# Two cache copies from DRAM to DRAM, issued in the third pair from the end and no longer among the first attention loads

## The chip, the cores and the metric

The kernel runs on one core of a Trainium2 chip. The metric is device time of one execution in microseconds (us). The engines are PE (matrix products), DVE (vector work), ACT (activations, copies and casts), POOL, and SP, which here does nothing but issue transfers. Each engine runs its own instructions in order; engines wait for one another and for transfers by semaphores.

## What is computed

One inference step of a hybrid layer on 1024 prompt tokens and on 8 samples of 4 tokens (32 sample tokens): 1024 features, an mLSTM branch with 4 heads and an attention branch with 8 query and 2 key/value heads of 64, over a window of 128 positions.

```
h = rmsnorm(x, g) * (1 + scale) + shift            # scale, shift, gate from c
mq, mk, mv, mi, mf, mo, mz, aq, ak, av, az, gm, ga = split_in(h @ w_in)
y_m, C, n, m = mlstm_branch(...)                   # gated by sigmoid(mo) * silu(mz)
k = partial_rope(ak); v = av
kk = concatenate([cache_k, k]); vv = concatenate([cache_v, v])      # samples
o = sink_attend(q, kk, vv, ...)
k_sample, v_sample = kk[:, -128:], vv[:, -128:]
y_a = o * silu(az)
x = x + gate * ((sigmoid(gm) * (y_m @ w_mo) + sigmoid(ga) * (y_a @ w_ao)) @ w_o)
```

The part that matters here is `k_sample` and `v_sample`: of each sample's 128 cached rows the last 124 are kept and its 4 new rows follow. Nothing in the step reads these two outputs again.

## The kernel before

**Products.** Matrix products in fp32 are made of two parts: each weight tile is split into a rounded part `wh` (a cast on ACT) and the rest `wl` (a subtraction on DVE), each input likewise into `h_h` and `h_l`, and three matmuls stand for one product: `h_h` with `wh`, `h_l` with `wh`, `h_h` with `wl`. Every matmul is recorded at L275, every instruction of ACT and DVE at L220, every transfer at L261 (`dma` and `issue`, L254 to L270).

**First stage.** Up to about 130 us PE makes the attention's projections (`g_aq` for the queries) column group by column group. Between them it runs side work, generators that are stepped when they are due. `kv_turn` (L797) is one: it turns the new values (`avn`, to DRAM as `vnD`), writes the outputs `v_p` and `k_p` and the samples' `k_s` and `v_s`. The queries go to DRAM (`qD<-aqr`), come back in the layout that attention needs (`uqv<-qD`, `ukv<-kD`, `uqv<-vnD`), and the first unit of attention multiplies them (`sc<-ukv,uqv`). In the same queue run the weights (`wr_aq`, `wr_mk`) and those of the conditioning (`adar_ga`).

**Pairs.** Then come 18 pairs of projection columns, by `block_products` (L1520): 4 of the mLSTM inputs, 8 gates, 2 of the attention's output gates, and 4 `head_gate` pairs, one per mLSTM head, each of one block of `mo` and one of `mz`. A pair takes seven products of weight combinations, in the order 5, 6, 2, 7, then product 1 of the next pair, then 3 and 4. A weight in the trace is named by its product (`wh_phead_gate_5` is product 5 of a `head_gate` pair) and a running number. Before each product `hook(n, i)` is called with the pair's number and the product's, and product 5 of a pair loads the four weight tiles of the next (`wr_mo` and `wr_mz`, two each, 256 KB a tile, from a ring of 9 buffers). `wh` and `wl` come from rings of 4 buffers each: a cast waits until PE has done with the tile four casts back.

Results lie in PSUM banks of four pools with 2 banks each. The pool `pg` holds `bx` and `bw`. Product 2 ends the use of `bx` (ACT takes the result out: `hg<-bx`), and product 1 of the next pair, two products later, writes the same bank again:

```
flat += [(n, i) for i in (5, 6, 2, 7)] + nx if n else ...
elif i == 2:
    job_.done(0, 0, X)          # hg<-bx
if i == 1:
    o = NX = bank(pg, "bx")
```

**Order.** PE's instructions are chained in the order of the code. In this stage the order on ACT, DVE and SP is made by a scheduler, from its own estimate of when each becomes ready, so that an instruction which moves can move others. Transfers are further held by `paced`: until the last but one pair, each SP transfer is put behind the PE instruction that stands last in the code when it is issued. The writes of results (`ymD<-hg`, `ymD<-gts`) are collected by `store` and issued 8 us of estimated PE time later; `ho<-yhD` loads what the mLSTM heads left in DRAM.

Of the kernel before, what the change touches and what calls it, by code (L numbers as in the profile page):

```python
# [173 lines left out]
def body(tc, a):  # L174
    nc = tc.nc
    with ExitStack() as ctx:
# [11 lines left out]
        def pb(shape, name):  # L188
            return ps.tile(shape, F32, tag="b", bufs=2, name=name)
# [4 lines left out]
        def ht(shape, name, dt=F32):  # L194
            return sp.tile(shape, dt, tag="half", bufs=50, name=name)
# [51 lines left out]
        def stores(src=None):  # L247

            for e in list(due):
                if e[0] <= side.now or (src is not None and e[1].tensor is src):  # L250
                    due.remove(e)
                    issue(*e[1:])

        def dma(out, in_, late=False):  # L254
            stores(in_.tensor)
            issue(out, in_, late)
# [3 lines left out]
        def issue(out, in_, late=False, eng=None):  # L260
            ins = (eng or nc.sync).dma_start(out, in_)  # L261
            ins = getattr(ins, "ins", ins)
            if eng is None and paced:
                no_sync(ins, [last["PE"]])
            if late:
                no_sync(ins, free)
                free.clear()
            free.append(ins)
# [8 lines left out]
        def tr(out, in_, idn):  # L277
            side.now += 0.11
            side.products += 1
            in_order(nc.tensor.transpose(out, in_, idn))  # L280
# [516 lines left out]
        def kv_turn():  # L797
            kl, kTs, vT, kns, vns = at.pop("kl"), at["kTs"], at.pop("vT"), ht([128, 128], "kns")[:NS], at["vns"]
            for p, n in enumerate((3, 3, 2)):
                tp = pb([128, 3, 128], f"vtp{p}")  # L800
                for j in range(n):
                    tr(tp[:, j], vT[p][:, j * 128:(j + 1) * 128], ident)
                vn = ht([128, 3, 128], f"avn{p}")
                S.copy(vn[:, :n], tp[:, :n])
                dma(vnD[:, 3 * p:3 * p + n], vn[:, :n])
                if p < 2:
                    yield 4.0, "b"
            dma(a["v_p"], vn[:, 1])
            tp = pb([128, 3, 128], "kvtp")
            tr(tp[:, 0], kl[:, 128:256], ident)  # L810
            tr(tp[:NS, 1], kTs, ident)
            tr(tp[:NS, 2], vT[2][:, 256:288], ident)
            kn = ht([128, 128], "kl")
            V.tensor_copy(kn, tp[:, 0])
            V.tensor_copy(kns, tp[:NS, 1])
            V.tensor_copy(vns, tp[:NS, 2])
            dma(a["k_p"], kn)
            dma(a["k_s"][0:124], a["cache_k"][4:128])
            dma(a["v_s"][0:124], a["cache_v"][4:128])
            dma(a["k_s"][124:128].rearrange("t b e -> b t e"), kns)  # L820
            dma(a["v_s"][124:128].rearrange("t b e -> b t e"), vns)

# [673 lines left out]
        class head_gate:  # L1496
# [14 lines left out]
            def samples(self, o):  # L1511
# [6 lines left out]
                store(ymD[h][:, SEQ:T], t[:, 0])  # L1518

        def block_products(jobs, hook):  # L1520
            flat = [(0, 1)]
            for n in range(len(jobs)):
# [25 lines left out]
            for j, (n, i) in enumerate(flat):  # L1548
                job_ = jobs[n]
                nxt = jobs[n + 1] if n + 1 < len(jobs) else None  # L1550
                hook(n, i)
                if i == 3 and not nxt:
                    job_.samples_end()
# [55 lines left out]
        def att_sums(k):  # L1609

            def part(n, t):
                if n in ROOM:
                    hi, lo = [y[:, ROOM.index(n), 512 * k:512 * k + 512] for y in ymt]
                else:
                    hi, lo = [ht([128, 512], f"ya{n}{x}{k}", F32R) for x in "hl"]
                ya[n][k] = hi, lo
                S.copy(hi, t)
                (G if (n, k) in ASIDE else V).tensor_tensor(lo, t, hi.bitcast(F32), op=ALU.subtract)

            ts = []  # L1620
            for i, f in ((k, 0), (2 + k, 1), (k, 1), (2 + k, 0)):
                ts.append(ht([128, 512], "yr"))
                dma(ts[-1], yaD[i][:, HALF[f]])
            b11, b22, b12, b21 = ts
            yield 6.0, ""
            src = {"b11": b11, "t2": b11, "b21": b21, "t4": b21, "b22": b22, "t3": b22, "t1": b12}
            less = {"t3": (b22, b12), "t1": (b12, b11), "t4": (b21, b11)}
            for n in (("b22", "t3", "b21", "b11", "t1", "t2", "t4"), ("b11", "b22", "t3", "t1", "t2", "b21", "t4"))[k]:
                while n in ROOM and not ymt:
                    yield 0.3, ""  # L1630
                if n in less:
                    x, y = less[n]
                    V.tensor_tensor(x, x, y, op=ALU.subtract)
                elif n == "t2":
                    V.tensor_tensor(b11, b11, b22, op=ALU.add)
                part(n, src[n])
                yield LAG, ""
# [289 lines left out]
        for p, (c0, n) in enumerate(PARTS):  # L1927
            if p == 2:
                dma(hD[:, :, SEQ:T], xS)
            else:  # L1930
                for k in range(KT):
                    dma(hD[:, k, c0:c0 + n], xT[p][k])
        side.add("m", gates(gp, zg, gbias), "")
        side.add("a", kv_turn(), "b")
        V.on = S.on = False
        paced.append(True)
# [84 lines left out]
        pairs = [Pair(head_in, i) for i in range(len(paired))] + [Pair(gate, d) for d in range(KT)] + [Pair(query_gate, i) for i in range(2)] + [Pair(head_gate, h) for h in range(NH)]  # L2021

        def hook(n, i):
            if n == 0 and i in (6, 5):
                side.until(lambda: {6: "t2", 5: "t1"}[i] in formed)
            if i == 6:
                if pairs[n].kind is query_gate:
                    side.until(lambda: len(units_done) == 16)
                side.until(lambda: len(samples_done) >= {head_in: 0, gate: 0, query_gate: 1, head_gate: pairs[n].i + 2}[pairs[n].kind])
            if (n, i) == (OUT_WEIGHTS, 6):  # L2030
                side.add("g", out_weights())
            if (n, i) in LOADS:
                side.add("x", att_sums(LOADS.index((n, i))))
            if n == len(pairs) - 1:
                next(att, None)
            if n == len(pairs) - 2:
                paced.clear()
            if (n, i) == (10, 7):
                begun.append(4)

        OUT_WEIGHTS = 5
        LOADS = [(len(pairs) - 2, 7), (len(pairs) - 1, 5)]
        work = block_products(pairs, hook)
        att = att_products()
        side.add("g", ada_gate())
# [163 lines left out]
        for i, r in enumerate(blocks_of_rows):  # L2209
# [69 lines left out]
            else:  # L2279
# [9 lines left out]
                for f, (y, (c0, n)) in enumerate(zip(Y, parts)):  # L2289
                    r.product(4, y, False, c0, n)  # L2290
                    c = slice(c0, c0 + n)
# [85 lines left out]
```

## Time and profile before

| | |
|---|---|
| median of the runs | 823.43 us (3 runs, 823.28 to 824.55) |
| the profiled execution | 823.38 us |
| its span, first to last instruction | 821.6 us |
| mean granted clock of PE | 0.997 |
| busy: PE, DVE, ACT, POOL | 803.5, 598.6, 419.5, 45.8 us |
| transfers, mean rate | 165.49 MB, 201 GB/s |
| the two copies | 496 KB each, issued at 72.37 and 80.33 us |

The times in the text are those of the profiled execution, counted from the start of its span. "PE 90%" in the profile's chain that ended last says that nine tenths of the time are a sequence of PE instructions; the rest of a view's columns are named where it is quoted. Matmuls overlap: one of 512 columns is recorded as 0.39 us long and the next begins 0.23 us behind its start.

### The profile page before, as it was taken

The numbers are of one execution on the slowest core, as the hardware profiler recorded it, in microseconds if no ns is written. First come the engines' busy times: TensorE is split into PE (matmuls) and PEld (weight loads), VectorE is DVE, ScalarE is ACT, GpSimd is POOL, SyncE is SP. The second block draws the span as 40 slices with busy tenths as digits, with TensorE's granted clock in tenths as the row PEclk, the third lists the DMA queues.
The fourth block names the chain that finished last, engine by engine and source line by source line (L and its number), as shares of the span: only waits on it lengthen the run. The fifth ranks groups of instructions, "written<-read, shape, count | busy, mean of one in ns | idle before, by whom it ended". The sixth has DMA issues, their size and how long they took to land.

```text
span 821.6 us, 15097 instructions
## 1 busy us (share of the span) xinstructions
PE 803.5 (98%) x5145; PEld 666.4 (81%) x5145; DVE 598.6 (73%) x1495; ACT 419.5 (51%) x1020; POOL 45.8 (6%) x111
## 2 busy tenths in 40 slices
PE   6999999999999999999999999999999999999996
PEld 3779898888788878888888878788888789997775
DVE  4799886756755557475657889898668997876666
ACT  5764355656565564546555545554446652224334
POOL 0120000000000000000001011010002101000000
PEclk9999999999999999999999999999999999999998
DMA  9995756546545415437765685864435789647632
GB/s 332 374 333 159 227 164 211 178 153 212 171 138 174 145 59 160 160 136 255 238 213 145 238 265 184 265 217 141 141 104 179 241 303 375 228 137 284 205 104 109
DMA packets 113473, 165.49 MB, mean 201 GB/s; under 512 B 21184, under 2 KB 55744, under 8 KB 113364
## 3 DMA queue, kind: packets, MB, share of 16 engines
q1 hardware_dynamic: 107748, 153.78, 56.9%
q10 hardware_dynamic: 4176, 6.56, 2.2%
q0 software_dynamic: 1472, 4.20, 1.4%
q8 instruction: 40, 0.66, 0.3%
q14 instruction: 37, 0.30, 0.1%
HBM read 115.51 MB, written 50.00 MB: 201 GB/s over the span
## 4 chain that ended last, share of the span: by engine, by line
PE 90%; DVE 5%; DMA 2%; issue 2%; ACT 1%; SPq 0%; DVEq 0%; ACTq 0%
PE by L275 12%; PE bx L275 11%; PE bw L275 11%; PE g_w_mo L275 6%; PE bz L275 5%; PE g_mq L275 3%; PE g_aq L275 3%; PE foW L275 3%; PE foX L275 2%; PE foY L275 2%; PE smp L275 2%; PE sc L275 2%; PE oT L275 2%; PE pt L280 2%; PE n L275 2%
## 5 line engine op out<-in xcount | busy, mean ns | idle before, releaser
L220 ACT ACTIVATE p<-p,nmx 128x256 f32<-128x256 f32 (+1 forms) x64 | 31.1, 486 | 17.7 <-DVE nmx L220 17.7
L220 DVE CUSTOM_DVE_ANT_0 p<-sc,cst,sink 128x256 f32<-128x256 f32 (+1 forms) x64 | 26.1, 462 | 9.2 <-PE sc L275 9.1
L275 PE MATMUL g_aq<-h_h,wh_aq 128*128 128x384 f32 (+1 forms) x96 | 32.2, 336 | 0.0
L275 PE MATMUL g_aq<-h_h,wl_aq 128*128 128x384 f32 (+1 forms) x96 | 30.9, 322 | 0.0
L275 PE MATMUL g_aq<-h_l,wh_aq 128*128 128x384 f32 (+1 forms) x96 | 30.9, 321 | 0.0
L275 PE MATMUL g_w_mo<-ym_h,wh_w_mo 128*128 128x384 f32 (+1 forms) x96 | 30.8, 321 | 0.0
L275 PE MATMUL g_w_mo<-ym_l,wh_w_mo 128*128 128x384 f32 (+1 forms) x96 | 30.8, 321 | 0.0
L275 PE MATMUL g_w_mo<-ym_l,wl_w_mo 128*128 128x384 f32 (+1 forms) x96 | 30.8, 321 | 0.0
L220 DVE COPY p<-pt 128x512 f32<-128x512 f32 (+1 forms) x16 | 10.5, 657 | 16.9 <-PE pt L280 16.8
L220 ACT CAST wosh<-wor 128x512 fp32r<-128x512 f32 x24 | 14.8, 621 | 12.6 <-DVE wor L220 12.6
L275 PEld LDWEIGHTS g_aq<-h_h,wh_aq 128*128 128x128 f32 x96 | 18.0, 188 | 2.5 <-issue 1.5
L261 POOL DMA_DIRECT2D oD<-uqv x16 | 8.8, 552 | 183.1 <-ACT uqv L220 169.9
L220 DVE SCALAR_TENSOR_TENSOR tgw_mo<-tgw_mo,g_w_mo 128x384 f32<-128x384 f32 (+1 forms) x24 | 12.4, 518 | 8.8 <-PE g_w_mo L275 7.9
L220 DVE TENSOR_TENSOR wosl<-wor,wosh 128x512 fp32r<-128x512 f32 x24 | 16.5, 686 | 2.8 <-ACT wosh L220 2.7
L275 PE MATMUL sc<-ukv,uqv 64*128 64x256 f32 (+1 forms) x128 | 18.0, 390 | 0.5 <-DMA ukv<-kD 0.5
L275 PEld LDWEIGHTS g_aq<-h_l,wh_aq 128*128 128x128 f32 x96 | 18.1, 188 | 0.0
L275 PEld LDWEIGHTS g_w_mo<-ym_l,wh_w_mo 128*128 128x128 f32 x96 | 18.0, 188 | 0.0
L275 PEld LDWEIGHTS g_w_mo<-ym_h,wh_w_mo 128*128 128x128 f32 x96 | 18.0, 188 | 0.0
L275 PEld LDWEIGHTS g_aq<-h_h,wl_aq 128*128 128x128 f32 x96 | 18.0, 188 | 0.0
L275 PEld LDWEIGHTS g_w_mo<-ym_l,wl_w_mo 128*128 128x128 f32 x96 | 18.0, 188 | 0.0
L220 DVE TENSOR_TENSOR et<-et,S 128x384 f32<-128x384 f32 (+1 forms) x12 | 6.1, 509 | 15.8 <-PE S L275 15.8
L275 PE MATMUL g_mq<-h_h,wh_mq 128*128 128x384 f32 (+1 forms) x48 | 16.8, 350 | 0.3 <-ACT mk L220 0.3
(2063 smaller groups left out, 2807.5 us busy)
## 6 DMA issues: line engine op xcount, KB each, us to landing
x<-xT SPq DMA_DIRECT2D x16, 256.0 KB
early_h<-w_ada SPq DMA_DIRECT2D x8, 512.0 KB
adar_ga<-w_ada SPq DMA_DIRECT2D x16, 256.0 KB
wr_ga<-w SPq DMA_DIRECT2D x16, 256.0 KB
wr_gm<-w SPq DMA_DIRECT2D x16, 256.0 KB
taD<-gt SPq DMA_DIRECT2D x16, 256.0 KB
tmD<-gt SPq DMA_DIRECT2D x16, 256.0 KB
wor<-w_out SPq DMA_DIRECT2D x16, 256.0 KB
```

What stands on the lines that cost most here:

```text
L220: ins = f(*args, **kw)
L261: ins = (eng or nc.sync).dma_start(out, in_)
L275: in_order(nc.tensor.matmul(out, lhsT, rhs, start=start, stop=stop, skip_group_check=more))
L280: in_order(nc.tensor.transpose(out, in_, idn))
```

## The change

The two copies leave `kv_turn` and are issued from `hook`: in pair 15 of 0 to 17 (`head_gate` of head 1, the third from the end), `cache_k` ahead of product 6 and `cache_v` ahead of product 2.

```diff
             dma(a["k_p"], kn)
-            dma(a["k_s"][0:124], a["cache_k"][4:128])
-            dma(a["v_s"][0:124], a["cache_v"][4:128])
             dma(a["k_s"][124:128].rearrange("t b e -> b t e"), kns)
             dma(a["v_s"][124:128].rearrange("t b e -> b t e"), vns)
...
             if n == len(pairs) - 2:
                 paced.clear()
+            if n == len(pairs) - 3 and i in (6, 2):
+                c = "kv"[i == 2]
+                dma(a[c + "_s"][0:124], a["cache_" + c][4:128])
             if (n, i) == (10, 7):
                 begun.append(4)
```

Running numbers differ by 2 in places (`wr_aq_0_1018` before is `wr_aq_0_1016` of the change). PE's order is the same in both. On three engines rows change places.

SP, first stage, from the weights' load ahead of the first copy to the loads of attention's first unit. Before:

```order
L261 DMA adar_ga_936<-w_ada 128x512
L261 DMA k_s<-cache_k 16x7936
L261 DMA vnD<-avn_967 128x256
L261 DMA v_p<-avn_967 128x128
L261 DMA k_p<-kl 128x128
L261 DMA v_s<-cache_v 16x7936
L261 DMA k_s<-kns 8x4x128
L261 DMA v_s<-vns 8x4x128
L261 DMA adar_ga_984<-w_ada 128x512
L261 DMA wr_aq_0_1018<-w 128x512
L261 DMA wr_aq_1_1020<-w 128x512
L261 DMA qD_114<-aqr 128x384 x2
```

And of the change:

```order
L261 DMA adar_ga_936<-w_ada 128x512
L261 DMA wr_aq_0_1016<-w 128x512
L261 DMA wr_aq_1_1018<-w 128x512
L261 DMA vnD<-avn_967 128x256
L261 DMA v_p<-avn_967 128x128
L261 DMA k_p<-kl 128x128
L261 DMA k_s<-kns 8x4x128
L261 DMA v_s<-vns 8x4x128
L261 DMA adar_ga_982<-w_ada 128x512
L261 DMA qD_114<-aqr 128x384 x2
L261 DMA uqv<-vnD 128x256
L261 DMA qD_114<-aqr 128x256
```

Both copies are gone, and the two `wr_aq` loads stand where `k_s<-cache_k` stood, no longer just ahead of `qD<-aqr`.

SP, in the pairs of heads 1 and 2, from the second load of head 2's weights on. Before:

```order
L261 DMA wr_mz_1_7096<-w 128x512
L261 DMA n_s<-n_5369 128x32
L261 DMA ho<-yhD_128 128x512
L261 DMA wr_mo_0_7274<-w 128x512
L261 DMA ho<-yhD_128 128x512
L261 DMA ymD_131<-hg_7018 128x512
L261 DMA wr_mo_1_7276<-w 128x512
L261 DMA wr_mz_0_7278<-w 128x512
L261 DMA wr_mz_1_7280<-w 128x512
L261 DMA ymD_131<-hg_7085 128x512
L261 DMA ymD_132<-gts 128x32
```

And of the change:

```order
L261 DMA n_s<-n_5367 128x32
L261 DMA k_s<-cache_k 16x7936
L261 DMA ho<-yhD_128 128x512
L261 DMA v_s<-cache_v 16x7936
L261 DMA ho<-yhD_128 128x512
L261 DMA ymD_131<-hg_7016 128x512
L261 DMA ymD_131<-hg_7083 128x512
L261 DMA ymD_132<-gts 128x32
L261 DMA wr_mo_0_7274<-w 128x512
L261 DMA wr_mo_1_7276<-w 128x512
L261 DMA wr_mz_0_7278<-w 128x512
L261 DMA wr_mz_1_7280<-w 128x512
```

The copies stand round the first `ho`, and the four weight loads of the last pair (7274 to 7280) stand behind the three writes to `ymD`.

ACT, at the end of head 1's pair, where the next pair's product 1 follows (weight 7141 is its `wh`; `gts` and `smps` belong to the samples; `ws` is a sum of weights). Before:

```order
L220 CAST wh_phead_gate_4__7212<-wr_mz_1_6882 128x512
L220 ACTIVATE hg_7158<-bx 128x512
L220 ACTIVATE gts<-smpo 128x64
L220 COPY smps<-smp 128x128
L220 CAST wh_phead_gate_5__7229<-ws_7187 128x512
L220 ACTIVATE hg_7207<-hg1z 128x512
```

And of the change:

```order
L220 CAST wh_phead_gate_4__7212<-wr_mz_1_6880 128x512
L220 ACTIVATE gts<-smpo 128x64
L220 CAST wh_phead_gate_5__7229<-ws_7187 128x512
L220 ACTIVATE hg_7158<-bx 128x512
L220 COPY smps<-smp 128x128
L220 ACTIVATE hg_7207<-hg1z 128x512
```

The cast of weight 7229 has moved ahead of `hg<-bx` and of `smps<-smp`. On DVE the subtraction for 7229 likewise moves ahead of `hg1z`, and the sum `ws_7370` of two of the last pair's weights (7278 and 7280) from ahead of the subtraction for 7253 to behind it.

## The prediction, made before the change was run

> **What bounds the kernel now.** I read the list of engines first, then the list of everything that the matrix engine (PE) waits for, then the timelines round the two places that the change touches.
>
> ```profile
> PE 803.5 (98%) x5145; PEld 666.4 (81%) x5145; DVE 598.6 (73%) x1495; ACT 419.5 (51%) x1020; POOL 45.8 (6%) x111
> ```
>
> The waits of PE (what waited, for what: us in total, times, longest):
>
> ```profile
> PE xc L275 <- ACT xsq L220: 6.6, 1, 6.6
> PE adat_q L275 <- ACT adas_q L220: 0.7, 1, 0.7
> PE xc L275 <- ACT xsum L220: 0.7, 1, 0.7
> PE bx L275 <- DVE zt L220: 0.7, 1, 0.7
> PE pt L280 <- DVE mx L220: 0.5, 1, 0.5
> PE sc L275 <- DMA ukv<-kD: 0.5, 1, 0.5
> PE g_mq L275 <- ACT mk L220: 0.3, 1, 0.3
> ```
>
> PE works 803.5 of 821.6 us. The other 18 us are 6.6 at the start, 7.9 of tail behind its last matmul (it ends at 813.72, below) and six waits of 0.3 to 0.7 us. So time can move by two things only: one of these waits goes, or PE gets a new one. A DMA that nobody on PE waits for is worth nothing here, whatever its size. Of the seven waits one is for a DMA, `sc` for `ukv<-kD`, and it lies just behind the place where the copies are issued now.
>
> **The early place: what the removal is worth.** First the chain of waits up to that `sc` (start, us, what).
>
> ```profile
> 84.06 5.35 DMA qD<-aqr
> ...
> 89.85 2.31 DMA ukv<-kD
> ```
>
> PE's timeline there and at the next unit (start, us, engine, line, operation, how many, and in brackets the idle time before it):
>
> ```profile
> 91.45 0.34 PE L275 MATMUL g_aq<-h_h,wl_aq 128*128 128x384 f32 x1
> 92.29 0.93 PE L275 MATMUL sc<-ukv,uqv 64*128 64x128 f32 x8 [0.50 <-DMA ukv<-kD]
> ...
> 101.57 0.34 PE L275 MATMUL g_aq<-h_h,wl_aq 128*128 128x384 f32 x1
> 101.84 1.14 PE L275 MATMUL sc<-ukv,uqv 64*128 64x256 f32 x8
> ```
>
> And SP's timeline, the queue that issues these transfers:
>
> ```profile
> 72.37 0.81 SPq L261 DMA_DIRECT2D k_s<-cache_k  x1
> ...
> 80.33 0.55 SPq L261 DMA_DIRECT2D v_s<-cache_v  x1
> 80.97 0.82 SPq L261 DMA_DIRECT2D k_s<-kns  x1
> ...
> 82.69 0.38 SPq L261 DMA_DIRECT2D adar_ga<-w_ada  x1
> 83.13 0.89 SPq L261 DMA_DIRECT2D wr_aq<-w  x2
> 84.06 1.45 SPq L261 DMA_DIRECT2D qD<-aqr  x3
> ```
>
> The reader is to see one serial path: SP issues `qD<-aqr` at 84.06, the data is in DRAM 5.35 us later, SP then issues `uqv<-qD` and `ukv<-kD`, and the last of them releases `sc` at 92.29. PE was free earlier. At the next unit, where nothing is waited for, `sc` begins 101.84 - 101.57 = 0.27 us behind the start of the last `g_aq`; here it would begin at 91.45 + 0.27 = 91.72. So 92.29 - 91.72 = **0.57 us** is all that can be had at this place (the list says 0.50, since it counts from the modelled end of the matmul).
>
> Does the change give all of it? Out of SP's queue ahead of `qD` go the issue of `v_s<-cache_v`, 80.97 - 80.33 = 0.64 us, and the two `wr_aq`, 84.06 - 83.13 = 0.93 us, which move up into the empty place that `k_s<-cache_k` leaves at 72.37 (in front of SP's long wait for `avn`, where 0.9 us of issuing hold up nothing). `qD` is issued 1.57 us earlier. If its landing still took 5.35 us, the chain would end 1.57 us sooner, 1.0 us before PE asks. With 1 MB less in the queue just ahead of it (496 KB of `v_s` and 512 KB of `wr_aq`) the landing will rather be shorter. Bounds: 0 if another input of `sc` is late instead, 0.57 at most, and below 0 only if the wait grew, which fewer bytes and an earlier issue exclude. I take 0.57, and PE itself is what comes last then. The six later waits of the list do not take it back: each begins with PE's own products, so it moves along. The other rows that change places between 100 and 113 us, on DVE and ACT, and a `wr_mk` load that is issued later, are done several us before PE asks for what they make: 0, and a few tenths like the waits of the list if one of them came last after all.
>
> **The late place: the copies themselves.** SP's queue there:
>
> ```profile
> 574.94 0.86 SPq L261 DMA_DIRECT2D wr_mo<-w  x2
> ...
> 583.67 0.33 SPq L261 DMA_DIRECT2D wr_mo<-w  x1
> ...
> 590.94 3.04 SPq L261 DMA_DIRECT2D wr_mz<-w  x2
> ...
> 595.24 0.33 SPq L261 DMA_DIRECT2D ymD<-gts  x1
> ```
>
> Two stretches of the same time (length, busy times of the engines, granted clock, share of the DMA engines, GB/s), and two casts of weights on ACT:
>
> ```profile
> 577.40:580.40 3.00, 3.00 (x15) 2.47 (x14) 1.40 (x3) 0.62 (x1) 0.00 (x0) 1.00 0.89 288
> 580.40:584.00 3.60, 3.60 (x18) 2.98 (x17) 2.38 (x4) 1.74 (x3) 0.00 (x0) 1.00 0.06 20
> ```
>
> ```profile
> 586.85 0.62 ACT L220 CAST wh_phead_gate__7141<-wr_mo 128x512 fp32r<-128x512 f32 x1 [1.59 <-issue]
> ...
> 607.30 0.62 ACT L220 CAST wh_phead_gate__7324<-wr_mo 128x512 fp32r<-128x512 f32 x1 [1.59 <-issue]
> ```
>
> The copies cost SP 0.81 + 0.55 us of issuing at about 577 to 579. The stretches show the loads ahead of them moving until 580.4, and then 3.6 us at a share of 0.06. At the 288 GB/s of the row above, the 992 KB of both copies take 3.5 us and fit there. What they could delay is the loads beside them, for a pair whose first cast is at 586.85, 6 us behind their landing. Cost 0; the whole 3.5 us in front of those loads would still cost 0.
>
> By the order, the last pair's four weight loads fall behind `ymD<-gts`, so from 583.67 to 593.98 (590.94 + 3.04) to about 595.24 + 0.37 = 595.6 and on. Four equal loads issued from 574.94 were in by 580.4, 5.5 us; these are then in by about 601.1. Their first casting reader on ACT is at 607.30. On DVE, `ws<-wr_mz,wr_mz` reads them (597.93 before, behind the subtraction of weight 7254 now, near 601). What stands behind `ws` on DVE is bounded under the rivals. Cost 0.
>
> **The late place: a cast that slips in front.** This is where I expect a loss. ACT's timeline before, then PE's:
>
> ```profile
> 592.28 0.62 ACT L220 CAST wh_phead_gate__7212<-wr_mz 128x512 fp32r<-128x512 f32 x1 [1.61 <-issue]
> 592.81 0.59 ACT L220 ACTIVATE hg<-bx 128x512 f32<-128x512 f32 x1
> ...
> 596.42 0.62 ACT L220 CAST wh_phead_gate__7229<-ws 128x512 fp32r<-128x512 f32 x1 [2.46 <-PE by L275]
> ```
>
> ```profile
> 595.96 0.39 PE L275 MATMUL by<-t3l,wh_phead_gate__7121 128*128 128x512 f32 x1
> ...
> 596.41 0.39 PE L275 MATMUL bx<-h_h,wh_phead_gate__7141 128*128 128x512 f32 x1
> ```
>
> The cast of weight 7229 waits 2.46 us for PE: its tile is the one that PE's `by` products read until 596.35 (595.96 + 0.39). Before, `hg<-bx` stood ahead of it and had emptied the `bx` bank of PSUM by 593.40. Now the cast stands ahead of `hg<-bx` (rows in the section on the change), so on an engine that works in order `hg<-bx` cannot run until PE has finished `by`. And PE's very next product, `bx<-h_h` with weight 7141, overwrites the bank that `hg<-bx` empties: in the code the two banks of that pool alternate, and this product waits for that row. So PE runs dry:
>
> - cast 596.42; the next ACT row begins 592.81 - 592.28 = 0.53 us behind such a cast: `hg<-bx` 596.95 to 597.54;
> - from the end of an ACT row to the PE matmul that waits for it 0.05 us (below: 13.00 - 12.37 - 0.58): 597.59;
> - PE would have begun at 596.41: a stall of **1.18 us**, new.
>
> ```profile
> 12.37 0.58 ACT L220 COPY xsum<-xs 128x512 f32<-128x512 f32 x1 [1.88 <-PE xs L275]
> ...
> 13.00 0.49 PE L275 MATMUL xc<-cst,xsum 128*128 128x1 f32 x3 [0.68 <-ACT xsum L220]
> ```
>
> Bounds: 0 if `hg<-bx` were not held after all; 1.18 otherwise, give or take 0.1 for a row or a hand-over that is longer. I take 1.18, since each term is a row of the same engine and shape. The other rows that slide (`smps<-smp` on ACT, `hg1z` and the subtraction of weight 7230 on DVE) are asked for by PE 5 us and more later. Nothing later gives the stall back: no PE wait stands behind 596 in the list, and everything from here on hangs on PE.
>
> **Sum**, on the profiled execution: 823.38 - 0.57 + 1.18 = **823.99**, so 824.0 us. The median of the runs before is 823.43, 0.05 more, well inside their spread (823.28 to 824.55). About 0.2%, 1.6 us, is what a measurement of this kernel can tell from no change; the forecast is +0.07%, no change in that sense: two small terms of opposite sign.
>
> **Rivals.**
>
> *The gain alone.* The ACT rows run as before in effect, say because `hg<-bx` is not what PE waits for: 823.38 - 0.57 = 822.8. For it: PE's list of before has no such wait. Against it: in both programs the `bx` product waits for just that row; before it was simply 3 us early. 0.07.
>
> *The stall alone.* `sc` stays late at 92, because the landing of `qD` stretches by 1.0 us or more though less lies ahead: 823.38 + 1.18 = 824.6. Against it: bytes and issue time both fall. 0.06.
>
> *Nothing moves*, the change does not do what it says: the copies keep colliding with something of the same weight and the cast falls in line: 823.4. 0.02.
>
> *Slower, by the weights.* DVE works in order, and behind `ws` now wait `hg<-p,bw` and the subtraction of weight 7283. DVE's row, and the PE row that it sets free:
>
> ```profile
> 602.05 0.69 DVE L220 TENSOR_TENSOR hg<-p,bw 128x512 f32<-128x512 f32 x1 [1.55 <-PE bw L275]
> ```
>
> ```profile
> 607.29 0.39 PE L275 MATMUL bw<-t2h,wh_phead_gate__7253 128*128 128x512 f32 x1
> ```
>
> `hg<-p,bw` empties the `bw` bank for the product that PE starts at 607.29, now 608.47 (`ws` to `hg<-p,bw` 0.60, as between two such rows on DVE, 0.69 for the row and 0.05 to hand over). If the weights land at T, the bank is free at T + 1.34. PE stalls from T = 607.1 on, one for one, and the total passes 825.0 from T = 608.1. I expect T = 601.1, so the loads would have to take 12.6 us in place of 5.5. At T = 609 the time is 823.99 + 1.9 = 825.9. For it: the loads are issued 12 us later than before. Against it: SP has nothing else of size queued there. 0.04.
>
> *Slower, by the clock.* If the stall of 1.18 us made the granted clock fall, PE would run at half rate for a while. PE's last row, and two stretches behind it (the clock is the third number from the end):
>
> ```profile
> 813.44 0.28 PE L275 MATMUL foY<-wosh,u3wl 128*128 128x256 f32 x1
> ```
>
> ```profile
> 815.50:816.00 0.50, 0.00 (x0) 0.00 (x0) 0.47 (x3) 0.00 (x0) 0.00 (x0) 1.00 0.11 37
> ...
> 816.50:817.00 0.50, 0.00 (x0) 0.00 (x0) 0.43 (x3) 0.00 (x0) 0.00 (x0) 0.50 0.00 0
> ```
>
> The last matmul ends at 813.72; the clock is whole up to 816.0 and half from 816.5 on. So it takes at least 2.3 us without a matmul, twice the stall. Were it half for the 5.1 us for which it is seen half here, PE would do 2.55 us less work: 826.5. 0.03. [...]
>
> **How the numbers follow.** Forecast 0.74, gain alone 0.07, stall alone 0.06, nothing 0.02, slower 0.04 + 0.03 and 0.01 for a further stall, 0.03 for a gain over 0.2% that I do not see. Faster 0.03, same 0.89, slower 0.08. The range runs from the gain alone, 822.8, to the stall alone (824.6) with some tenths for the spread of the runs before, 824.9; it leaves out 0.11.
>
> **What would show it.** Right: no `sc` wait for `ukv<-kD` near 92, `qD` issued near 82.5; a new PE wait of `bx` for ACT `hg` of about 1.2 us (some 0.9 if counted from the modelled end) near 596; `k_s` and `v_s` issued near 577 to 579, the last pair's weights near 595.6 and in by 601; the six other waits as they are. Wrong: `sc` still waiting at 92, `hg<-bx` done by 594, or a DVE wait for `wr_mz` that reaches 607.

## The result, and the profile of the changed kernel

The changed kernel takes 824.69 us (median of 21 runs, 824.32 to 825.9), the kernel before beside it 823.60 us (median of 21, 822.95 to 824.55): a ratio of **1.0015, 95% interval 1.0009 to 1.0021**, so 1.1 us more, between 0.7 and 1.7. That is within 0.2%, as forecast (824.0), and a little more on the slow side than forecast. The profiled execution took 824.55 us, its span 822.7.

The list of what PE waits for (what waited, for what: us in total, times, longest) shows what came and what went:

```profile
PE xc L275 <- ACT xsq L220: 5.7, 1, 5.7
PE bx L275 <- ACT hg L220: 1.0, 1, 1.0
PE g_mq L275 <- ACT aq L220: 0.9, 1, 0.9
```

The wait of `sc` for `ukv<-kD` is gone, the wait of `bx` for `hg` is new and as foretold, and one more is new that was not foretold: `g_mq` for ACT's `aq`. (`xc` at the start is not the change's: PE begins its first product somewhere between 5.7 and 7.1 us, in any kernel here.)

PE's timeline at the first place:

```profile
91.13 0.34 PE L275 MATMUL g_aq<-h_h,wl_aq 128*128 128x384 f32 x1
91.40 0.93 PE L275 MATMUL sc<-ukv,uqv 64*128 64x128 f32 x8
```

`sc` starts 0.27 us behind the last `g_aq`, as at the units that never waited; before it was 0.84. The gain in this pair of profiles is the 0.57 us of the sum. SP's timeline shows why:

```profile
72.06 1.22 SPq L261 DMA_DIRECT2D wr_aq<-w  x2
...
82.25 0.89 SPq L261 DMA_DIRECT2D qD<-aqr  x2
...
85.50 0.32 SPq L261 DMA_DIRECT2D uqv<-qD  x1
85.87 0.42 SPq L261 DMA_DIRECT2D ukv<-kD  x1
...
577.52 0.63 SPq L261 DMA_DIRECT2D k_s<-cache_k  x1
...
578.82 0.54 SPq L261 DMA_DIRECT2D v_s<-cache_v  x1
...
595.87 0.86 SPq L261 DMA_DIRECT2D wr_mo<-w  x2
596.78 0.90 SPq L261 DMA_DIRECT2D wr_mz<-w  x2
```

`qD` is issued 1.8 us earlier than before (0.3 of it is the earlier start of PE), and it is in after 3.2 us, not 5.35, so `ukv<-kD` goes out 4 us earlier. The copies and the last pair's weights stand where the order puts them.

The late place, ACT's timeline and then PE's:

```profile
592.50 0.62 ACT L220 CAST wh_phead_gate__7212<-wr_mz 128x512 fp32r<-128x512 f32 x1 [1.61 <-issue]
...
596.64 0.62 ACT L220 CAST wh_phead_gate__7229<-ws 128x512 fp32r<-128x512 f32 x1 [3.40 <-issue]
597.16 0.59 ACT L220 ACTIVATE hg<-bx 128x512 f32<-128x512 f32 x1
```

```profile
596.40 0.39 PE L275 MATMUL by<-t3h,wl_phead_gate__7121 128*128 128x512 f32 x1
597.81 0.50 PE L275 MATMUL bx<-h_h,wh_phead_gate__7141 128*128 128x512 f32 x1 [1.02 <-ACT hg L220]
598.14 0.39 PE L275 MATMUL bx<-h_l,wh_phead_gate__7141 128*128 128x512 f32 x1
```

ACT sits for 3.4 us with `hg<-bx` ready to run behind the cast that is not. PE would have begun `bx` at 596.40 + 0.23 = 596.63 and begins at 597.81: 1.18 us, to the hundredth what was worked out. (The profile puts the cast's wait down to "issue" here; before it named PE's `by`, and the cast still starts only when the last `by` product that reads its tile has ended, 596.17 + 0.39.) What the sum left out is the start behind a wait: the first matmul takes 0.50 us and not 0.39, and the next begins 0.33 us behind it and not 0.23.

The third place, 123 us. The end of the chain of waits (start, us, what), then ACT's and DVE's timelines:

```profile
120.61 1.46 PE g_aq L275 x11
122.07 0.56 ACT p L220
122.63 0.39 ACT aq L220
123.02 0.04 issue
123.06 0.45 PE g_mq L275
```

```profile
117.00 0.37 ACT L220 COPY uqv<-oT 128x256 f32<-128x256 f32 x1 [3.53 <-PE oT L275]
117.27 0.62 ACT L220 CAST t3h<-x 128x512 fp32r<-128x512 f32 x1
118.73 0.51 ACT L220 ACTIVATE p<-p,nmx 128x256 f32<-128x256 f32 x1 [0.84 <-DVE nmx L220]
...
122.53 0.47 ACT L220 ACTIVATE aq<-g_aq 128x384 f32<-128x384 f32 x1
```

```profile
117.92 0.69 DVE L220 TENSOR_TENSOR t3l<-x,t3h 128x512 fp32r<-128x512 f32 x1 [0.56 <-ACT t3h L220]
118.53 0.16 DVE L220 TENSOR_SCALAR nmx<-mx 128x4 f32<-128x4 f32 x1
```

And the same rows of ACT before:

```profile
112.53 0.61 ACT L220 CAST t3h<-x 128x512 fp32r<-128x512 f32 x1
117.91 0.37 ACT L220 COPY uqv<-oT 128x256 f32<-128x256 f32 x1 [4.78 <-PE oT L275]
118.18 0.51 ACT L220 ACTIVATE p<-p,nmx 128x256 f32<-128x256 f32 x1
...
121.98 0.48 ACT L220 ACTIVATE aq<-g_aq 128x384 f32<-128x384 f32 x1
```

Before, the cast `t3h` ran at 112.53, long before `uqv<-oT`. In the change it stands behind `uqv<-oT`, which waits for PE until 117.0. So DVE's `t3l` waits for `t3h`, `nmx` stands behind `t3l`, ACT's `p<-p,nmx` waits for `nmx`, and at the end of ACT's queue `aq<-g_aq` empties the bank that `g_mq` wants. It starts at 122.53, against 121.98 before, although PE is 0.9 us ahead by then.

### The profile page after: what moved, and what is told of

It reads as the page before. It is cut to its first block, busy times and chain, and to the rows that moved or that the text cites. A ratio compares the mean times of both kernels' runs of the same rounds, so it can differ in the third digit from the quotient of the medians.

```text
span 822.7 us, 15098 instructions
## 1 busy us (share of the span) xinstructions
PE 804.0 (98%) x5145; PEld 666.4 (81%) x5145; DVE 598.5 (73%) x1495; ACT 419.4 (51%) x1020; POOL 45.8 (6%) x111
## 4 chain that ended last, share of the span: by engine, by line
PE 91%; DVE 3%; issue 2%; DMA 2%; ACT 1%; SPq 0%; DVEq 0%; ACTq 0%
PE bx L275 11%; PE by L275 11%; PE bw L275 11%; PE g_aq L275 6%; PE g_w_mo L275 6%; PE bz L275 5%; PE foW L275 3%; PE g_mq L275 3%; PE foX L275 2%; PE foY L275 2%; PE smp L275 2%; PE sc L275 2%; PE oT L275 2%; PE n L275 2%; PE pt L280 2%
## 5 line engine op out<-in xcount | busy, mean ns | idle before, releaser
L220 ACT ACTIVATE p<-p,nmx 128x256 f32<-128x256 f32 (+1 forms) x64 | 31.0, 486 | 18.2 <-DVE nmx L220 18.0
L220 DVE CUSTOM_DVE_ANT_0 p<-sc,cst,sink 128x256 f32<-128x256 f32 (+1 forms) x64 | 26.1, 463 | 9.2 <-PE sc L275 9.1
L275 PE MATMUL g_aq<-h_h,wh_aq 128*128 128x384 f32 (+1 forms) x96 | 32.2, 336 | 0.0
L275 PE MATMUL g_aq<-h_h,wl_aq 128*128 128x384 f32 (+1 forms) x96 | 30.9, 322 | 0.0
L275 PE MATMUL g_aq<-h_l,wh_aq 128*128 128x384 f32 (+1 forms) x96 | 30.8, 321 | 0.0
L275 PE MATMUL g_w_mo<-ym_l,wh_w_mo 128*128 128x384 f32 (+1 forms) x96 | 30.8, 321 | 0.0
L275 PE MATMUL g_w_mo<-ym_h,wh_w_mo 128*128 128x384 f32 (+1 forms) x96 | 30.8, 321 | 0.0
L275 PE MATMUL g_w_mo<-ym_l,wl_w_mo 128*128 128x384 f32 (+1 forms) x96 | 30.8, 321 | 0.0
L220 DVE COPY p<-pt 128x512 f32<-128x512 f32 (+1 forms) x16 | 10.5, 656 | 15.6 <-PE pt L280 15.6
L220 ACT CAST wosh<-wor 128x512 fp32r<-128x512 f32 x24 | 14.8, 621 | 12.6 <-DVE wor L220 12.6
L275 PEld LDWEIGHTS g_aq<-h_h,wh_aq 128*128 128x128 f32 x96 | 18.0, 188 | 2.6 <-issue 1.5
L220 DVE SCALAR_TENSOR_TENSOR tgw_mo<-tgw_mo,g_w_mo 128x384 f32<-128x384 f32 (+1 forms) x24 | 12.4, 519 | 8.7 <-PE g_w_mo L275 7.9
L220 DVE TENSOR_TENSOR wosl<-wor,wosh 128x512 fp32r<-128x512 f32 x24 | 16.5, 686 | 2.9 <-ACT wosh L220 2.7
L275 PE MATMUL g_mq<-h_h,wh_mq 128*128 128x384 f32 (+1 forms) x48 | 16.9, 352 | 1.2 <-ACT aq L220 0.9
L275 PEld LDWEIGHTS g_w_mo<-ym_l,wh_w_mo 128*128 128x128 f32 x96 | 18.0, 188 | 0.0
L275 PEld LDWEIGHTS g_aq<-h_l,wh_aq 128*128 128x128 f32 x96 | 18.0, 188 | 0.0
L275 PEld LDWEIGHTS g_w_mo<-ym_h,wh_w_mo 128*128 128x128 f32 x96 | 18.0, 188 | 0.0
L275 PE MATMUL sc<-ukv,uqv 64*128 64x256 f32 (+1 forms) x128 | 18.0, 390 | 0.0
L275 PEld LDWEIGHTS g_w_mo<-ym_l,wl_w_mo 128*128 128x128 f32 x96 | 18.0, 188 | 0.0
L275 PEld LDWEIGHTS g_aq<-h_h,wl_aq 128*128 128x128 f32 x96 | 18.0, 188 | 0.0
L220 DVE TENSOR_TENSOR et<-et,S 128x384 f32<-128x384 f32 (+1 forms) x12 | 6.1, 510 | 15.8 <-PE S L275 15.8
```

The costliest lines, as they stand in the source:

```text
L220: ins = f(*args, **kw)
L275: in_order(nc.tensor.matmul(out, lhsT, rhs, start=start, stop=stop, skip_group_check=more))
```

## The experiments

The times of different profiles differ at the start and elsewhere by luck (in the four profiles of before PE waits 5.7 to 6.7 us for its first product, and they part by up to 0.21 us behind 630), so beside the time I compare PE's matmuls one by one: the start of the k-th matmul in a profile less its start in the first profile of before. This difference is flat over hundreds of matmuls, and a step in it is what a place costs (medians over the stretches between the places; us):

| kernel | early copies | step at sc | step at 123 | step at 597 | behind 630 |
|---|---|---|---|---|---|
| before (first profile) | yes | 0 | 0 | 0 | 0 |
| before, three more | yes | +0.40, +0.19, +0.41 | 0, 0, -0.02 | 0, 0, +0.02 | -0.03, +0.06, +0.18 |
| changed | no | -0.59 | +1.13 | +1.34 | -0.37 |
| changed, once more | no | -0.59 | +1.10 | +1.33 | -0.24 |
| early row put back | no | -0.60 | +0.46 | +1.33 | -0.50 |
| late row put back | no | -0.59 | +1.11 | +0.02 | -0.65 |
| both rows put back | no | -0.59 | +0.48 | +0.02 | -0.27 |
| three rows put back | no | -0.59 | +0.03 | +0.01 | -0.62 |
| copies left out | no | -0.60 | +1.12 | 0 | -0.03 |
| late copies to scratch | yes | -0.53 | -0.02 | +0.02 | -0.04 |
| v alone, by POOL | k | -0.60 | 0 | +0.02 | -0.04 |
| k left out | v | -0.60 | -0.01 | +0.01 | -0.22 |

My theory after the result: the time follows the order of a few rows on ACT and DVE, and the transfers cost nothing where they are now. The rival: the bytes, or the loads that moved with them, cost what was lost. In the listings of the runs that put rows back, a helper line shifts L220 to L221 and L275 to L276. A row is put back by an order-only dependency between two rows of one engine.

**The early row.**

```diff
-            S.copy(hi, t)
+            first[n, k] = S.copy(hi, t)
...
+            if (g, b0) == (0, 0):
+                no_sync(raw_ins(c), [raw_ins(first["t3", 2])])
```

> The changed kernel with one row of ACT put back: the cast t3h stands ahead of uqv<-oT again (116 us), all else as changed. If the order of the ACT rows makes the new wait of g_mq for aq at 123 us (0.87 us, 1.01 us of PE time), it goes and the late wait of bx for hg (1.02 us) stays: 1.0 us less than the changed kernel, +0.6 against the kernel before. Rival, the loads that moved with the copies make it (transfers arriving in another order): the wait at 123 stays at 0.9 and the time at +1.6 less the luck of the start.

Measured: 824.09 us, ratio 1.0005 (0.9996 to 1.0014). PE's timeline at 122 us:

```profile
122.07 0.29 PE L276 MATMUL g_aq<-h_h,wl_aq 128*128 128x288 f32 x1
122.60 0.44 PE L276 MATMUL g_mq<-h_h,wh_mq 128*128 128x384 f32 x1 [0.23 <-ACT aq L221]
```

The wait falls from 0.87 to 0.23 and the step from 1.13 to 0.46. So this row made most of it, not the loads, but not all: 0.46 stay.

**The late row.**

```diff
+            if name == "phead_gate2_5_":
+                no_sync(raw_ins(c), [raw_ins(first["hg0"])])
```

> The changed kernel with the other row put back: on ACT hg<-bx stands ahead of the cast of weight 7229 again, the copies and the loads of the last pair stay where the change puts them. If the order makes the stall, the bx wait of 1.02 us near 597 goes, 1.18 us less than the changed kernel, +0.45 against the kernel before, and the wait at 123 stays. Rival, the bytes of the copies or the later weight loads make the loss there: PE stalls near 597 to 610 all the same, about 1 us in all, and the time is that of the changed kernel.

Measured: 823.40 us, ratio 0.9995 (0.9986 to 1.0004). PE's timeline:

```profile
597.01 0.39 PE L276 MATMUL by<-t3h,wl_phead_gate__7121 128*128 128x512 f32 x1
597.23 0.39 PE L276 MATMUL bx<-h_h,wh_phead_gate__7141 128*128 128x512 f32 x1
```

`bx` follows `by` by 0.22 us, with the copies at 578 to 580 and the last pair's weights at 596.5 as in the changed kernel. The stall was that row; on DVE `hg1z` went back ahead of the subtraction for 7229 together with it.

**Both rows, and the copies left out.**

> Both rows put back. By the order theory only the gain at sc is left: -0.56 against the kernel before, about 823.0, no PE wait at 92, 123 or 597. By the rival (bytes and loads cost something in one of the two places) between 0 and +1.6.

> The two copies are left out altogether (rows 0 to 123 of the samples' k and v outputs are not written); the early rows are those of the changed kernel, the late rows of ACT those of the kernel before. By the order theory -0.56 at sc and +1.01 at 123, no wait at 597: +0.45, the same as with the late row alone put back, though 1 MB less is moved. If the bytes cost something, it is faster than that one by their cost.

Measured: 822.87 us with both rows, ratio 0.9990 (0.9981 to 0.9999), and 824.38 without copies, ratio 1.0007 (0.9998 to 1.0015). Moving 1 MB less gained nothing at any of the places: the steps are those of the rows alone. The time itself missed what was expected: it should have equalled that of the late row put back and is 1.0 us longer. Of this 0.62 lies behind 630 and 0.16 behind PE's last matmul; the rest is not found. With both rows back the chain of waits at 123 ran from `g_mq` back through ACT's `aq` and `p<-p,nmx` to DVE's `ropet`, which waited for an earlier `aq<-g_aq`; and that one stood on ACT behind `p<-p,den`, which needs the last row of this piece of DVE's timeline:

```profile
110.88 0.54 DVE L221 COPY p<-pt 128x384 f32<-128x384 f32 x1
...
112.09 0.18 DVE L221 RECIPROCAL den<-den 128x4 f32<-128x4 f32 x1
```

Before, the same two rows stood the other way round:

```profile
109.88 0.16 DVE L220 RECIPROCAL den<-den 128x4 f32<-128x4 f32 x1
...
112.87 0.55 DVE L220 COPY p<-pt 128x384 f32<-128x384 f32 x1
```

**A third row, the reciprocal ahead of the copy.**

```diff
+                    if (g, b0) == (0, 0):
+                        no_sync(raw_ins(c), [raw_ins(first["den", 2])])
```

> Both ACT rows put back as in the run before, and one row of DVE: the reciprocal of unit 2's denominators ahead of the copy p<-pt. With both ACT rows back PE still waited 0.2 us for aq at 123 (0.38 us of PE time), and there the chain ran back through aq<-g_aq, which stood behind p<-p,den on ACT, to that reciprocal at 111.92. If this row makes the rest of the wait, it begins near 111.5, the wait of g_mq for aq goes and the step at 123 is 0 to 0.1: -0.5 against the kernel before. Rival, the gain at sc simply uses up the slack that aq had (0.43 us before): the step stays near 0.3 to 0.4 whatever the row.

Measured: **822.55 us, ratio 0.9985 (0.9976 to 0.9994)**, by its median the fastest of the kernels with both copies late. PE's timeline:

```profile
122.76 0.29 PE L276 MATMUL g_aq<-h_h,wl_aq 128*128 128x288 f32 x1
122.89 0.40 PE L276 MATMUL g_mq<-h_h,wh_mq 128*128 128x384 f32 x1
```

No wait, a step of 0.03. The reciprocal began at 112.36, not near 111.5 as I wrote; but PE began 0.69 us later in that execution, so against PE it is 0.42 earlier, and that was enough. The rest of the wait was that row; the slack of `aq` was not used up by the gain.

**The copies once more, late, with the old rows.** The kernel before, and in `hook` two copies to unused DRAM:

```diff
+            if n == len(pairs) - 3 and i in (6, 2):
+                c = "kv"[i == 2]
+                dma(twice[c, 0], a["cache_" + c][4:128])
```

> The kernel before, with the early copies as they were, and the same two copies once more in the late place, into DRAM that nothing reads (1 MB more is moved). SP's order there is like the changed kernel's for the copies, and the rows of ACT are those of the kernel before, all of them. By the order theory PE's steps are 0 everywhere: same time within 0.1. By the rival (the copies' bytes and their place in SP's queue cost something in the late place) PE falls back there by up to 1.2 us.

Measured: 823.85 us, ratio 1.0004 (0.9995 to 1.0012). Two stretches round the copies (length, busy times of PE, PEld, DVE, ACT, POOL, granted clock, share of the DMA engines, GB/s), and PE's timeline:

```profile
577.00:580.00 3.00, 3.00 (x14) 2.45 (x14) 1.55 (x3) 0.63 (x2) 0.00 (x0) 1.00 1.12 396
580.00:584.00 4.00, 4.00 (x19) 3.32 (x18) 2.59 (x4) 1.85 (x4) 0.00 (x0) 1.00 0.75 250
```

```profile
595.94 0.39 PE L275 MATMUL by<-t3h,wl_phead_gate__7125 128*128 128x512 f32 x1
596.16 0.39 PE L275 MATMUL bx<-h_h,wh_phead_gate__7145 128*128 128x512 f32 x1
```

The DMA engines are at a share of 1.12 until 580 and of 0.75 until 584, and PE is busy in every us and steps nowhere in the late place. But there is a surprise in the early one: with the early copies in place and the early rows of before, `sc` did not wait in the profiled execution: it starts at 92.10, 0.33 us behind the last `g_aq`. The time does not show this gain: the median is 0.3 us above that of before beside it.

**v alone, by POOL, and k left out.**

```diff
+                issue(a["v_s"][0:124], a["cache_v"][4:128], eng=nc.gpsimd, src_late=True)
```

> Only the copy of cache_v is moved, and POOL issues it, late. ACT and DVE have exactly the rows of the kernel before, SP too but for the one issue that is gone. sc gains its 0.56 (qD issued 0.64 earlier, behind 496 KB less); at 123 between 0 and 0.13 of it is lost, since aq had 0.43 of slack; nothing at 597: -0.43 to -0.56 against the kernel before. If POOL's issue or the late bytes cost something, it shows as a PE step behind 530.

> Only the copy of cache_k is left out (rows 0 to 123 of k_sample are not written); cache_v is copied early, in its place at 72.4. ACT and DVE as before. If the late sc hangs on SP's queue, the issue that is gone from between k_p and k_s<-kns (0.64 us) is enough: sc gains 0.5 to 0.56. If it hangs on the bytes, the gain depends on whether 496 KB at 72 or at 80 us stood in the way; with the bytes at 72 still there it is as large, without them no larger.

Measured: 822.84 us, ratio 0.9992 (0.9983 to 1.0000), with v by POOL (issued at 558.81); and 822.46 in one run without k. Either copy out of the early queue is enough for the whole gain at `sc`, and with the old rows nothing of it is lost at 123. In both, one copy is left, near 72, and what stood at 80.3 is gone, its issue (0.64 us) and its 496 KB. SP's timeline with v by POOL:

```profile
83.24 1.43 SPq L261 DMA_DIRECT2D qD<-aqr  x3
...
87.53 0.32 SPq L261 DMA_DIRECT2D uqv<-qD  x1
```

Against PE's own work, `qD` is issued 0.62 to 0.65 us earlier in the two than in the first profile of before. And `uqv<-qD`, which waits for its landing, follows it by 4.29 us (4.57 without k), against 5.04 to 5.88, 5.55 in the mean, in the five profiles with both copies early. So the shorter landing gives more than the earlier issue. That the missing bytes make it shorter fits this but is not shown: no run takes away the bytes and leaves the issue.

**The kernels again.** One profile had carried the whole gain, so before was profiled three times more and the changed kernel once.

> The kernel before, profiled once more. In its first profile sc waited 0.50 us for ukv<-kD; in the run with the late scratch copies, with the same early rows and the same early copies, it did not wait (qD landed in 4.98 us, not 5.35). If that wait belongs to the kernel before, it is there again, 0.3 to 0.6; if it is the luck of one landing, it is anywhere from 0 to 0.6, and the gain that was taken from one profile is too large.

> The kernel before, profiled a third time (a comment line is added, nothing else). As in the run ahead of it: a wait of sc of 0.3 to 0.6 if it belongs to the kernel, anything from 0 on if it is luck.

> The kernel before, profiled a fourth time, for the same question, and for the stretch of 640 to 657 us, which took 0.43 us longer in three of ten profiles: that too should come and go if it is luck.

> The changed kernel, profiled once more. The waits that come from the order of rows stay to within 0.1: bx for hg 1.02, g_mq for aq 0.87; sc does not wait. The start of PE's work and the stretch of 640 to 657 us may differ by some tenths, as between the other profiles.

Measured: 823.82, 823.96, 824.27 and 825.76 us, one run each. PE's rows at `sc` in the three, in this order:

```profile
91.55 0.34 PE L275 MATMUL g_aq<-h_h,wl_aq 128*128 128x384 f32 x1
92.79 0.71 PE L275 MATMUL sc<-ukv,uqv 64*128 64x128 f32 x6 [0.91 <-DMA ukv<-kD]
```

```profile
91.82 0.34 PE L275 MATMUL g_aq<-h_h,wl_aq 128*128 128x384 f32 x1
92.87 0.71 PE L275 MATMUL sc<-ukv,uqv 64*128 64x128 f32 x6 [0.71 <-DMA ukv<-kD]
```

```profile
91.79 0.34 PE L275 MATMUL g_aq<-h_h,wl_aq 128*128 128x384 f32 x1
93.07 0.49 PE L275 MATMUL sc<-ukv,uqv 64*128 64x128 f32 x4 [0.94 <-DMA ukv<-kD]
```

The wait belongs to the kernel before, but its length is luck, the draw of one execution: over the five profiles with these early rows and both copies early, PE lost 0.57, 0.97, 0.78, 1.01 and 0.06 us to it (start of `sc` less start of the last `g_aq`, less 0.27), 0.68 in the mean. The waits that hang on the order of rows came out alike in both profiles of the changed kernel (0.9 and 1.0 in both lists). The stretch behind 630 varies too.

## Why the prediction came out right, and where it was wrong

The class was right, and so was the picture of two small terms of opposite sign; the net of +0.6 was smaller than the +1.1 (0.7 to 1.7) measured, and by its own steps this is why.

- *The gain at `sc`, 0.57.* Right in mechanism and for the profile that it was read from. Over five profiles the loss was 0.68 in the mean and between 0.06 and 1.01, so the one profile was no bound: "0.57 us is all that can be had" holds for that execution only.
- *The other rows between 100 and 113 us, cost 0.* **This step failed.** I compared when each moved row's own product was ready with when PE asks for it. What moved was a row, `t3h`, whose product is not urgent at all, to a place in front of rows that are: behind `uqv<-oT`, it holds up `t3l`, `nmx`, `p` and `aq`, in the order of two engines. The step is +1.12, of which the `t3h` row made 0.67 and the reciprocal's row 0.43 (0.46 left with the first put back, 0.03 with both). My bound of "a few tenths", taken from waits of 0.3 to 0.7, was too low. The lists in the section on the change show none of these early rows of ACT and DVE.
- *A cast that slips in front, 1.18.* Right, with the row, the wait and the size; the start behind the wait adds some 0.15, for a step of 1.33.
- *The copies themselves, 0.* Right: with ACT's old rows and 1 MB more in the late place PE steps nowhere, and without any copies the steps stay. They did keep the DMA engines busy there (a share of 0.81 between 580.4 and 584 in the changed kernel, 0.06 before), and PE waited for none of it.
- *The last pair's weights, 0.* Right: issued at 595.9 to 597.7, and `ws` on DVE ran at 601.97 behind the subtraction of weight 7254 without waiting for them.
- *Nothing gives the stall back.* Not quite: behind 630 the six profiles whose late rows and late loads are those of the change, or the change's with the cast put back, are 0.24 to 0.65 us better than the first profile of before, and the other eight lie between -0.22 and +0.18. In that group one DVE row, `hg<-hg,by`, stands ahead of the subtraction for product 7, on the way to a product at 633 (`by`) that waits for ACT in some profiles (0.2 to 0.7 us in six of them). That this row makes the difference is argued and not shown; no run moved it alone.

The steps of the changed kernel add up to -0.68 + 1.12 + 1.33 - 0.3 = +1.5, inside the measured interval.

That the time fell inside the range is partly luck. Every sign named for the two foretold places came, but the third place was priced at 0, and the range reached up to 824.9 only to take in the stall alone. Without the 0.3 that came back behind 630, for a reason that is still open, the same steps end at 823.38 + 1.8 = 825.2, outside it.

The rivals: none of them came; the weights did not hold DVE, and the clock stayed whole through the stall of 1.18 us:

```profile
597.00:599.00 2.00, 1.19 (x5) 1.02 (x6) 1.29 (x2) 1.30 (x4) 0.00 (x0) 1.00 0.82 265
```

## What to carry to other kernels

Where a scheduler decides the order, moving a transfer can cost more through the rows that change places (1.12 and 1.33 us here) than through its bytes (no step of PE here): for each moved row, look at what now stands behind it on its own engine, and follow that chain to the busiest engine, not only at who reads the row's product. In the two places here it reached PE through a PSUM bank that is emptied by a row behind a waiting one. And a wait for a transfer, read from one profile, is a draw (0.06 to 1.01 us in five profiles here): profile twice before a gain is counted on it.

## What the runs showed of the hardware

The landing time of one transfer behind others differs between executions of the same program: in the four profiles of before, SP issued `uqv<-qD` 5.41 to 5.88 us behind `qD`, and the wait that hangs on it cost PE 0.57 to 1.01 us. With the late scratch copies, whose program has the same early rows and transfers, it was 5.04 and 0.06 us.

Behind the stall at 597 the first matmul of 512 columns was recorded 0.50 us long and the next began 0.33 us behind it, against 0.39 and 0.23 in the flow.

The granted clock fell at 816.26 in the first profile of before, 2.5 us behind the last matmul, and later in the changed kernel, whose last matmul ends at 814.90:

```profile
818.00:819.00 1.00, 0.00 (x0) 0.00 (x0) 0.93 (x3) 0.69 (x1) 0.00 (x0) 0.88 0.00 0
819.00:820.00 1.00, 0.00 (x0) 0.00 (x0) 0.06 (x1) 0.03 (x1) 0.00 (x0) 0.50 0.06 23
```

A mean of 0.88 over the first stretch puts the fall from 1.00 to 0.50 at about 818.76, 3.9 us behind the last matmul. Over all fourteen profiles this gap runs from 2.04 us (the second repeat of before, mean granted clock 0.996 over 822.2 us) to 4.98 (k left out, 0.998 over 820.7 us), so the "at least 2.3 us" of the prediction, read from one profile, is no bound. In the traces' records of the clock the stretch at 1.00 is 805.545 us long in the first profile of before and 808.959 in that of the changed kernel: 3.41 us longer, where the last matmul ends 1.2 us later.

The record of the clock begins at 10.71 us in the first profile of before and at 9.80 in that of the changed kernel, and ahead of it the views print 1.00. That is no measured clock: in the first profile of before matmuls of 512 columns (`xs<-xsq,one`) are 1.04 to 1.06 us long up to 9.3 us and 0.59 to 0.62 from 10.76 on.
